# Weight splits moved off GpSimd, index steps charged less, the last selection's ends on GpSimd, masks one block ahead, chained minima

## The chip, the cores and the metric

The kernel runs as one program on one core of a Trainium2 chip. The metric is the device time of one execution in microseconds (us). TensorE does the matmuls, VectorE (DVE), ScalarE (ACT) and GpSimd (POOL) the element-wise work, and SyncE (SP) issues most of the transfers.

## The reference

One residual block on x (1 x 2048 x 1024, float32). A joint projection gives queries, a shared latent key and value, the indexer's queries, weights and keys, the pooling branch's input and two gates. For each block of 128 queries the indexer scores all admissible keys, and attention sees the 256 best alone:

```python
rel = jax.nn.relu(jnp.einsum('bqhd,bsd->bqhs', qib, k_idx).astype(jnp.float32) * idx_scale)
idx_score = jnp.einsum('bqh,bqhs->bqs', wib.astype(jnp.float32) * head_w_scale, rel)
idx_score = jnp.where(admissible[None], idx_score, -jnp.inf)
_, sel = lax.top_k(idx_score, topk)
...
s = jnp.einsum('bqhd,bqkd->bqhk', qb, k_sel).astype(jnp.float32) * attn_scale
p = jax.nn.softmax(s, axis=-1).astype(v_sel.dtype)
...
branch_a = attn @ w_attn_branch[l]
branch_b = multiscale_pool(pool_in, w_pool[l], pool_scale[l]) @ w_pool_branch[l]
gate_a, gate_b = jnp.split(jax.nn.sigmoid(gate_logits), 2, axis=-1)
mixed = (gate_a * branch_a + gate_b * branch_b) @ w_out[l]
x = layer_norm(ALPHA * x + mixed, ln1_g[l], ln1_b[l])
ffn = conv_ffn(x, conv_w[l], conv_b[l], w_ffn_up[l], w_ffn_down[l])
x = layer_norm(ALPHA * x + ffn, ln2_g[l], ln2_b[l])
```

There are 8 heads of 128 latent dimensions, 16 query blocks, and chunks of 64 frames; a query sees the keys of its own and of earlier chunks.

## The kernel before

**Matmuls.** Each float32 product is three matmuls: an operand is split into a rounded part `hi` and a rest `lo`, and `mm3` adds hi·hi, hi·lo and lo·hi. A split is two operations: a cast (`hi`) and a subtraction (`lo = src - hi`). `split` puts the cast on ACT and the subtraction on VectorE, or with `pool=True` both on GpSimd.

**Stages, in the order of the program.** The 2048 rows are four groups g of 512 (four blocks of 128 each). `proj_index` makes the indexer's and the latent projections of all groups (7.8 to 219.6 us). Then, for each group, `proj_pool`, `proj_q` and `proj_gates` (with `pool_map` inside): row group 0 from 219.6 to 438.9, group 1 to 664.2, group 2 to 902.5, group 3 to 1083.6. Attention runs over 32 units (g, h), a row group and a head each: those of group 0 until 1130.5, of group 1 until 1224.9, of group 2 until 1407, of group 3 until 1589.6. Then come `mix_out` (to 1870), `ffn_up` (to 2742) and `ffn_down`.

**Weights.** `self.ab` holds the projections' weights as tiles of 128x1024. The first row group loads each raw tile, splits it and stores both parts to DRAM; the later groups load the finished parts. In `get(i)`, tiles i+1 and i+2 are being loaded while tile i+1 is split. `self.ab` is made with the default `pool=True`, so its splits are on GpSimd: 32 tiles, of which 2 fall before 219.6 and 30 into the stage of row group 0.

**The background.** Index scores and selection are generators in `self.bg`, for the groups (0, 1), (2,) and (3,). After each step of the main program `turn` lets them go on as long as the modelled backlog of VectorE and ACT over TensorE (class `Clocks`) is under `SLACK`, and as long as there is credit, which grows by `RATE` = 0.75 of TensorE's modelled time and is charged by each step's modelled time on VectorE or ACT, whichever is longer. All of this is decided when the program is written out, so the order of instructions on each engine is fixed.

**Selection.** `index_scores` adds up the heads' scores of a block, one step for a head and a span. `select` then searches the 256th largest score of each row by bisecting over 32 bits, for two halves of the blocks in turn: a count on VectorE (`cd`, a compare that adds up), a sign sum on ACT (`ca`), and three small steps in `decide` (`g`, `h`, `F`) on 2 or 4 columns. The end of each block handles ties: ACT writes signs `sg` (f16), VectorE compares them with zero (`eq`), scans (`cu`), compares the scan with the number wanted, subtracts, and writes the mask (bf16, 0 or `MASKED`), which goes to DRAM through `self.stores`. The last selection is that of group 3, blocks 12 to 15 with 1664, 1792, 1920 and 2048 columns.

**Attention.** `load_unit(u + 1)` is called at the start of unit u's scores. For the first unit of a group it calls `load_masks(g)`: for each block of the group, `self.selected < b` steps the background by force until the mask is there, `settle` issues the waiting stores, and the mask is loaded; masks 0 and 1 are memsets on GpSimd. In `scores`, for each block rb and each chunk of up to 1024 keys, VectorE adds the mask to the scores in PSUM and takes the row maximum into `mx`; for a block of two chunks the maxima are joined and scaled by one operation on a column, for a block of one chunk they are scaled, and a memset clears the second sum. ACT then takes the exponential. `split_q(u + 1)` (on GpSimd) comes at the third block of a unit.

## Time and profile before

| | before |
|---|---|
| median of 3 runs | 3179.35 us (3173.73 to 3184.88) |
| profiled execution | 3178.85 us, span 3177.1 us |
| mean granted TensorE clock | 0.986 of full speed |
| TensorE busy | 3042.5 us (96%) |
| VectorE busy | 2486.0 us (78%) |
| ACT busy | 1587.3 us (50%) |
| GpSimd busy | 644.4 us (20%) |

Busy times are those of the one profiled execution; they overlap, and are means over stages that differ. The span is the time between the first and the last instruction on the core.

### The profile page before, as it was taken

How to read it: one execution, taken by the hardware profiler on the slowest of the kernel's cores; microseconds unless marked ns; L12 is line 12 of the kernel's file. 1: busy time of each engine (PE TensorE's matmuls, PEld its weight loads, DVE VectorE, ACT ScalarE, POOL GpSimd, SP SyncE). 2: the span in 40 equal slices, each digit the busy share in tenths (PEclk: the TensorE clock that was granted, in tenths of full speed). 3: DMA queues.
4: the chain of work that ended last, by engine and by line, in shares of the span. 5: the costliest groups of instructions: out<-in, count | busy, mean ns of one | idle time of the engine just before them, and what ended most of it. 6: DMA issues, size and time to landing. Idle time of an engine off the chain costs nothing. (4 is left out here: it accounts for less than half of the span.)

```text
span 3177.1 us, 44106 instructions
## 1 busy us (share of the span) xinstructions
PE 3042.5 (96%) x14750; PEld 2534.0 (80%) x14750; DVE 2486.0 (78%) x4737; ACT 1587.3 (50%) x3051; POOL 644.4 (20%) x592
## 2 busy tenths in 40 slices
PE   8988899999999999779999999999999999999998
PEld 8886688888888888668877777888778888888886
DVE  4589987987699989988876578999986655657776
ACT  3465656874578877657711134444443222433253
POOL 2027520010010221101231234545411111100011
PEclk9999899999999999989999999999999999999999
DMA  6658784756367332131254778888888866998753
GB/s 248 238 190 277 252 322 147 271 209 222 119 246 274 112 107 82 59 107 54 80 207 171 256 271 284 295 295 286 303 298 321 318 216 220 363 399 327 266 192 110
DMA packets 325841, 715.89 MB, mean 225 GB/s; under 512 B 27434, under 2 KB 132334, under 8 KB 325614
## 3 DMA queue, kind: packets, MB, share of 16 engines
q1 hardware_dynamic: 316974, 697.34, 61.9%
q10 hardware_dynamic: 8640, 15.73, 1.3%
q8 instruction: 117, 1.92, 0.2%
q14 instruction: 110, 0.90, 0.1%
HBM read 454.85 MB, written 258.11 MB: 224 GB/s over the span
## 5 line engine op out<-in xcount | busy, mean ns | idle before, releaser
L133 PE MATMUL p<-b,b 128*128 128x512 f32 (+3 forms) x12568 | 2825.4, 381 | 92.0 <-ACT b L133 32.0
L133 PEld LDWEIGHTS p<-b,b 128*128 128x128 f32 x12568 | 2254.6, 190 | 534.5 <-ACT b L133 35.6
L133 DVE TENSOR_TENSOR b<-p,b 128x512 f32<-128x512 f32 (+3 forms) x622 | 393.4, 655 | 154.6 <-PE p L133 98.1
L133 ACT ACTIVATE b<-p 128x512 fp32r<-128x512 f32 (+11 forms) x634 | 360.7, 603 | 280.6 <-PE p L133 268.9
L133 ACT ACTIVATE m<-b,F 128x448 bf16<-128x448 f32 (+3 forms) x448 | 366.2, 820 | 89.6 <-DVE F L133 70.9
L133 ACT ACTIVATE b<-b 128x512 fp32r<-128x512 f32 (+3 forms) x310 | 237.7, 784 | 325.6 <-DVE b L133 140.9
L133 DVE TENSOR_SCALAR_CACHE_REDUCE m<-b,F 128x512 bf16<-128x512 f32 (+6 forms) x476 | 370.1, 808 | 1.0
L133 DVE TENSOR_TENSOR b<-b,b 128x1024 fp32r<-128x1024 f32 (+6 forms) x268 | 302.9, 1141 | 76.0 <-DMA b<-h 29.9
L133 POOL TENSOR_TENSOR b<-b,b 128x1024 f32<-128x1024 f32 (+3 forms) x94 | 226.8, 2415 | 493.1 <-DVE b L133 339.8
L133 DVE SCALAR_TENSOR_TENSOR b<-b,cw,b 128x1023 f32<-128x1023 f32 (+1 forms) x176 | 246.3, 1412 | 69.7 <-ACT b L133 68.7
L133 ACT ACTIVATE b<-m 128x512 fp32r<-128x512 f32 x215 | 133.2, 628 | 334.7 <-DVE m L133 123.1
L133 ACT ACTIVATE b<-b,cw 128x1024 f32<-128x1024 f32 x88 | 106.9, 1236 | 269.9 <-DVE b L133 269.9
L133 ACT ACTIVATE b<-b,mx 128x1024 f32<-128x1024 f32 (+2 forms) x192 | 171.6, 896 | 73.0 <-DVE mx L133 71.2
L133 PE MATMUL p<-ident,b 128*128 128x128 f32 x1248 | 194.5, 274 | 9.6 <-DVE b L133 7.2
L133 DVE SCALAR_TENSOR_TENSOR b<-b,ws,b 128x768 f32<-128x768 f32 (+5 forms) x154 | 155.6, 1039 | 49.1 <-ACT b L133 46.8
L133 DVE CUSTOM_DVE_ANT_0 b<-p,b 128x1024 f32<-128x1024 f32 (+2 forms) x192 | 173.7, 907 | 20.9 <-PE p L133 19.9
L133 DVE TENSOR_TENSOR b<-m,b 128x512 fp32r<-128x512 f32 x215 | 151.2, 711 | 49.0 <-ACT b L133 48.8
L133 PEld LDWEIGHTS p<-ident,b 128*128 128x128 f32 x1248 | 152.4, 141 | 43.4 <-DVE b L133 5.1
L133 PE MATMUL p<-kst,b 128*128 128x384 f32 (+3 forms) x656 | 149.7, 359 | 6.8 <-DVE b L133 4.6
L133 ACT ACTIVATE m<-p 128x512 f32<-128x512 f32 (+2 forms) x172 | 100.8, 586 | 74.4 <-PE p L133 69.6
L133 PEld LDWEIGHTS p<-kst,b 128*128 128x128 f32 x656 | 111.9, 189 | 28.5 <-ACT b L133 13.7
L133 POOL TENSOR_SCALAR b<-b 128x1024 fp32r<-128x1024 f32 (+2 forms) x50 | 53.1, 1065 | 352.1 <-DMA b<-in_w_in_dram 184.9
(126 smaller groups left out, 1628.2 us busy)
## 6 DMA issues: line engine op xcount, KB each, us to landing
b<-wk SPq DMA_DIRECT2D x339, 512.0 KB
wk<-b SPq DMA_DIRECT2D x211, 512.0 KB
b<-h SPq DMA_DIRECT2D x88, 512.0 KB
b<-in_w_ffn_up_dram SPq DMA_DIRECT2D x44, 512.0 KB
h<-b SPq DMA_DIRECT2D x44, 512.0 KB
b<-vv SPq DMA_DIRECT2D x80, 256.0 KB
hs<-b SPq DMA_DIRECT2D x33, 512.0 KB
b<-hs SPq DMA_DIRECT2D x33, 512.0 KB
```

The source lines that it names most:

```text
L133: return f(*args, **kw)
```

## The change

- `self.ab` is made with `pool=False`: the first row group's weights are split by ACT (cast) and VectorE (subtraction).
- The steps of `index_scores` yield `LIGHT`, and `turn` charges such a step `RATE / INDEX_RATE`, 0.79 of its modelled time. This moves the background's later steps too.
- `select` gets the engine of the ends' element-wise operations: GpSimd for the selection of group 3, VectorE for the others. The scan, and the two operations on one column behind it, stay on VectorE.
- `load_masks(g)` becomes `load_mask(b)`: a block's mask is asked for while the block ahead of it is scored, in the first unit of a group, or for a group's first block in the last unit of the group before.
- The row maxima become minima of negated scores: the reduction scales by -`SCALE` and starts from the value of the chunk before, so that its last value is the bias of the exponential. The operation that joined and scaled them, the memset of the second sum, and for blocks of one chunk the addition of the two sums are gone.

```diff
--- before.py
+++ after.py
@@ -68,8 +68,10 @@
 NFIRST = 1
 FINE = "fine"
 PAUSE = "pause"
+LIGHT = "light"
 GRAIN = 1
 RATE = 0.75
+INDEX_RATE = 0.95
 CAP = 1.5
 EARLY = 2
 SWITCH = "A--"
@@ -449,7 +451,8 @@
                 self.bg.pop(0)
             if step == PAUSE:
                 break
-            self.credit -= max(work["dve"] - before["dve"], work["act"] - before["act"])
+            spent = max(work["dve"] - before["dve"], work["act"] - before["act"])
+            self.credit -= spent * (RATE / INDEX_RATE if step == LIGHT else 1.0)
 
     def run_to_end(self, gen):
         for step in gen:
@@ -548,7 +551,7 @@
         self.nab = len(specs) // NG
-        self.ab = Weights(self, specs, period=self.nab)
+        self.ab = Weights(self, specs, pool=False, period=self.nab)
 
 
     def load_x(self, g, n=DC // 2):
@@ -1042,11 +1045,11 @@
                         nc.vector.tensor_scalar(tiles[t], rl, wsc, None, op0=OP.mult)
                     else:
                         nc.vector.scalar_tensor_tensor(tiles[t], rl, wsc, tiles[t], op0=OP.mult, op1=OP.add)
-                    yield
+                    yield LIGHT
...
-    def select(self, halves):
+    def select(self, halves, ties):
@@ -1138,17 +1141,17 @@
                 nc.scalar.activation(sg[:, :N - w], front[b], AF.Sign, bias=tn[:, i:i + 1])
                 nc.scalar.activation(sg[:, N - w:], back[b], AF.Sign, bias=tn[:, i:i + 1])
                 yield
-                nc.vector.tensor_scalar(eq, sg, 0.0, None, op0=OP.is_equal)
+                ties.tensor_scalar(eq, sg, 0.0, None, op0=OP.is_equal)
                 nc.vector.tensor_tensor_scan(cu, eq, eq, 0.0, op0=OP.add, op1=OP.max)
                 nd = self.sml([P, 1], tag="nd")
                 nc.vector.scalar_tensor_tensor(nd, cu[:, N - 1:N], fx[:, i:i + 1], cg[:, i:i + 1],
                                                op0=OP.mult, op1=OP.subtract)
                 nc.vector.tensor_scalar(nd, nd, float(TOPK), None, op0=OP.add)
                 yield
-                nc.vector.tensor_scalar(eq, cu, nd, None, op0=OP.is_gt)
-                nc.vector.tensor_tensor(sg, sg, eq, op=OP.subtract)
+                ties.tensor_scalar(eq, cu, nd, None, op0=OP.is_gt)
+                ties.tensor_tensor(sg, sg, eq, op=OP.subtract)
                 m = self.T([P, N], BF16)
-                nc.vector.tensor_scalar(m, sg, -0.25, MASKED, op0=OP.is_lt, op1=OP.mult)
+                ties.tensor_scalar(m, sg, -0.25, MASKED, op0=OP.is_lt, op1=OP.mult)
                 self.store(self.d_msk[b], m)
                 del self.I[b]
                 self.selected = max(self.selected, b)
@@ -1169,28 +1172,26 @@
         self.kh, self.kl = [a, e], [b, f]
         self.masks, self.vv = {}, {}
 
-    def load_masks(self, g):
-        nc = self.nc
-        t = []
-        for b in range(g * RB, (g + 1) * RB):
-            m = self.T([P, P * (b + 1)], BF16)
-            if b < 2:
-                nc.gpsimd.memset(m, 0.0)
-                nc.gpsimd.memset(m[0:64, P * (b + 1) - 64:], MASKED)
-            else:
-                while self.selected < b:
-                    if next(self.bg[0][1], "end") == "end":
-                        self.bg.pop(0)
-                self.settle()
-                nc.sync.dma_start(m, self.d_msk[b])
-            t.append(m)
-        self.masks[g] = t
+    def load_mask(self, b):
+
+        nc = self.nc
+        if b >= NB or b in self.masks:
+            return
+        m = self.T([P, P * (b + 1)], BF16)
+        if b < 2:
+            nc.gpsimd.memset(m, 0.0)
+            nc.gpsimd.memset(m[0:64, P * (b + 1) - 64:], MASKED)
+        else:
+            while self.selected < b:
+                if next(self.bg[0][1], "end") == "end":
+                    self.bg.pop(0)
+            self.settle()
+            nc.sync.dma_start(m, self.d_msk[b])
+        self.masks[b] = m
 
     def load_unit(self, u):
 
         g, h = self.units[u]
-        if g not in self.masks:
-            self.load_masks(g)
         q = self.M([P, G])
         self.nc.sync.dma_start(q, self.d_q[g][:, h * ROT:(h + 1) * ROT])
         self.qraw[u] = q
@@ -1213,6 +1214,7 @@
         nc = self.nc
         g, h = self.units[u]
         if u == 0:
+            self.load_mask(0)
             self.load_unit(0)
             self.split_q(0)
         if u + 1 < len(self.units):
@@ -1224,7 +1226,9 @@
             b = g * RB + rb
             N = P * (b + 1)
             npc = (N + 1023) // 1024
-            m = self.masks[g][rb]
+            m = self.masks[b]
+            if h == 0 and rb < RB - 1 or h == H - 1 and rb == RB - 1:
+                self.load_mask(b + 1)
             if rb == 2 and u + 1 < len(self.units):
                 self.split_q(u + 1)
             qh, ql = (qs[:, i, rb * P:(rb + 1) * P] for i in range(2))
@@ -1236,25 +1240,25 @@
                     cw = min(512, n - c)
                     self.mm3(ps[:, c:c + cw], qh, ql, self.kh[pc][:, c:c + cw], self.kl[pc][:, c:c + cw], True, True)
                 s = self.T([P, n])
-                nc.vector.tensor_tensor_reduce(s, ps[:, :n], m[:, pc * 1024:pc * 1024 + n], scale=1.0, scalar=-3e38,
-                                               op0=OP.add, op1=OP.max, accum_out=mx[:, pc:pc + 1])
+                nc.vector.tensor_tensor_reduce(s, ps[:, :n], m[:, pc * 1024:pc * 1024 + n], scale=-SCALE,
+                                               scalar=mx[:, pc - 1:pc] if pc else 3e38,
+                                               op0=OP.add, op1=OP.min, accum_out=mx[:, pc:pc + 1])
                 ps_.append((s, n))
                 if pc < npc - 1:
                     yield n / (4.0 * P)
-            if npc == 2:
-                nc.vector.tensor_scalar(mx[:, 0:1], mx[:, 0:1], mx[:, 1:2], -SCALE, op0=OP.max, op1=OP.mult)
-            else:
-                nc.vector.tensor_scalar(mx[:, 0:1], mx[:, 0:1], -SCALE, None, op0=OP.mult)
-                nc.vector.memset(st["sum"][:, rb, 1:2], 0.0)
             for pc, (s, n) in enumerate(ps_):
-                nc.scalar.activation(s, s, AF.Exp, bias=mx[:, 0:1], scale=SCALE, accum_out=st["sum"][:, rb, pc:pc + 1])
+                nc.scalar.activation(s, s, AF.Exp, bias=mx[:, npc - 1:npc], scale=-1.0, accum_out=st["sum"][:, rb, pc:pc + 1])
             st["p"].append([s for s, _ in ps_])
             yield n / (4.0 * P)
         r = st["r"] = self.sml([P, RB], tag="rinv", bufs=10)
-        nc.vector.tensor_tensor(r, st["sum"][:, :, 0], st["sum"][:, :, 1], op=OP.add)
-        nc.vector.reciprocal(r, r)
+        if npc == 2:
+            nc.vector.tensor_tensor(r, st["sum"][:, :, 0], st["sum"][:, :, 1], op=OP.add)
+            nc.vector.reciprocal(r, r)
+        else:
+            nc.vector.reciprocal(r, st["sum"][:, :, 0])
         if h == H - 1:
-            del self.masks[g]
+            for b in range(g * RB, (g + 1) * RB):
+                del self.masks[b]
 
     def values(self, u):
 
@@ -2014,7 +2018,7 @@
             yield from self.index_scores(g)
         blocks = [b for g in groups for b in range(g * RB, (g + 1) * RB) if b >= 2]
         h = len(blocks) // 2 if len(blocks) < 4 else 2
-        yield from self.select([blocks[:h], blocks[h:]])
+        yield from self.select([blocks[:h], blocks[h:]], self.nc.gpsimd if groups[-1] == NG - 1 else self.nc.vector)
 
     def run(self):
         self.rows, self.wi_parts, self.keyed, self.selected = {}, [], -1, 1
```

What moves is shown at three places. In the rows, `b` are large tiles, `m` middle ones, `msk71` to `msk74` the masks of blocks 12 to 15 in DRAM, `q`, `vv`, `at` and `gm` queries, values, attention's output and gates in DRAM.

On SP in attention, before, around the start of group 3 (the value loads of unit 22, then the masks):

```order
L1204 DMA b4762_15750<-vv12_113 128x512
L1204 DMA b4763_15753<-vv13_114 128x512
L461 DMA msk71_172<-b4816_15962 128x1664
L1195 DMA m4846_16041<-q54_155 128x1x512
L1185 DMA b4815_15959<-msk71_172 128x1664
L461 DMA msk72_173<-b4822_15979 128x1792
L1185 DMA b4817_15966<-msk72_173 128x1792
L461 DMA msk73_174<-b4839_16020 128x1920
L1185 DMA b4823_15983<-msk73_174 128x1920
L461 DMA msk74_175<-b4845_16037 128x2048
```

and in the changed program at the start of attention, then, as the second piece, at the start of group 3:

```order
L1196 DMA m3944_12642<-q51_152 128x1x512
L1196 DMA m3946_12647<-q51_152 128x1x512
L464 DMA msk71_172<-b3939_12632 128x1664
L1205 DMA b3947_12649<-vv11_112 128x512
L1196 DMA m3970_12732<-q51_152 128x1x512
L1189 DMA b3953_12663<-msk61_162 128x384
L1189 DMA b3957_12674<-msk62_163 128x512
L1196 DMA m3993_12792<-q51_152 128x1x512
```

```order
L1205 DMA b4844_15866<-vv13_114 128x512
L1189 DMA b4883_16021<-msk71_172 128x1664
L1196 DMA m4896_16075<-q54_155 128x1x512
L464 DMA at77_178<-m4882_16017 128x512
L1205 DMA b4897_16077<-vv11_112 128x512
L1205 DMA b4897_16077<-vv12_113 128x512
L1205 DMA b4898_16080<-vv13_114 128x512
L1205 DMA b4898_16080<-vv14_115 128x512
L1189 DMA b4900_16084<-msk72_173 128x1792
L1189 DMA b4912_16131<-msk73_174 128x1920
```

The stores of the four last masks no longer stand between their own loads: that of block 12 stands ahead of the loads of masks 2 and 3, and the loads of masks 12 to 15 are apart, with other transfers between them.

On GpSimd at the start of attention, before (`b3851` and `b3852` split the latent keys, the memsets write masks 0 and 1, the rows on `m` split queries):

```order
L133 TENSOR_SCALAR b3851_12415<-b3795_12240 128x1024
L133 TENSOR_TENSOR b3852_12416<-b3795_12240,b3851_12415 128x1024
L133 MEMSET b3885_12525 128x128
L133 MEMSET b3886_12528 128x256
L133 MEMSET b3885_12525 64x64
L133 MEMSET b3886_12528 64x64
L133 TENSOR_SCALAR b3900_12565<-m3891_12540 128x512
L133 TENSOR_TENSOR b3900_12565<-m3891_12540,b3900_12565 128x512
```

and in the changed program:

```order
L135 TENSOR_SCALAR b3922_12544<-b3867_12368 128x1024
L135 TENSOR_TENSOR b3923_12545<-b3867_12368,b3922_12544 128x1024
L135 TENSOR_SCALAR b3934_12594<-b3933_12593 128x1664
L135 TENSOR_SCALAR b3934_12594<-b3935_12595,nd3938_12615 128x1664
L135 TENSOR_TENSOR b3933_12593<-b3933_12593,b3934_12594 128x1664
L135 TENSOR_SCALAR b3939_12632<-b3933_12593 128x1664
L135 MEMSET b3943_12639 128x128
L135 MEMSET b3943_12639 64x64
L135 MEMSET b3949_12652 128x256
L135 MEMSET b3949_12652 64x64
L135 TENSOR_SCALAR b3958_12676<-m3946_12647 128x512
L135 TENSOR_TENSOR b3958_12676<-m3946_12647,b3958_12676 128x512
L135 TENSOR_SCALAR b3941_12635<-b3940_12634 128x1792
```

The four element-wise operations of block 12's end stand ahead of the memsets of masks 0 and 1 and of the first query split; the first comparison of block 13 is behind that split.

On GpSimd in the stage of row group 0, before (rows of 128x1024 are splits of weights, the others belong to the pooling windows):

```order
L133 TENSOR_TENSOR b1090_3666<-b1028_3496,b1089_3665 128x1024
L133 TENSOR_SCALAR b1091_3669<-b1029_3498 128x1024
L133 TENSOR_TENSOR b1092_3670<-b1029_3498,b1091_3669 128x1024
L133 TENSOR_SCALAR b1157_3849<-b1087_3661 128x1024
L133 TENSOR_TENSOR b1158_3850<-b1087_3661,b1157_3849 128x1024
L133 TENSOR_SCALAR b1159_3853<-b1088_3663 128x1024
```

and on VectorE in the same stage, in the changed program (rows with `cd` are the search's counts; `g`, `h` and `F` its small steps):

```order
L135 TENSOR_SCALAR m1059_3553,cd1056_3550<-b628_1927,F1048_3515 128x128
L135 SCALAR_TENSOR_TENSOR g1060_3556<-cd1042_3507,ca1043_3508 128x4
L135 TENSOR_SCALAR h1061_3557<-g1060_3556 128x4
L135 SCALAR_TENSOR_TENSOR F1062_3558<-h1061_3557,F1039_3493 128x4
L135 TENSOR_SCALAR m1075_3590,cd1056_3550<-b650_2005,F1048_3515 128x256
L135 TENSOR_TENSOR b1066_3565<-b995_3381,b1065_3564 128x1024
L135 SCALAR_TENSOR_TENSOR g1080_3601<-cd1056_3550,ca1057_3551 128x2
L135 TENSOR_SCALAR m1079_3598,cd1076_3595<-b677_2132,F1062_3558 128x192
L135 TENSOR_TENSOR b1068_3569<-b996_3383,b1067_3568 128x1024
L135 TENSOR_SCALAR m1084_3612,cd1076_3595<-b747_2446,F1062_3558 128x320
L135 TENSOR_SCALAR h1081_3602<-g1080_3601 128x2
L135 TENSOR_SCALAR m1086_3617,cd1076_3595<-b779_2586,F1062_3558 128x448
L135 SCALAR_TENSOR_TENSOR F1082_3603<-h1081_3602,F1048_3515 128x2
```

The subtractions of the weights' splits now stand between the counts of the search on VectorE; their casts stand on ACT between the search's sign steps.

## Rows read from the trace of the kernel before

**Rows 1.** Windows by stage: window, length; busy us (count) by engine; PE clock, DMA share, GB/s.

```profile
90.90:219.60 128.70, 117.81 (x835) 110.49 (x834) 84.73 (x190) 66.02 (x130) 9.09 (x6) 0.97 0.54 182
219.60:438.90 219.30, 192.64 (x814) 152.74 (x813) 202.46 (x637) 142.57 (x428) 120.42 (x92) 0.95 0.82 287
461.60:532.10 70.50, 70.50 (x353) 59.02 (x352) 49.65 (x68) 32.28 (x49) 14.17 (x11) 1.00 0.48 171
902.50:1083.60 181.10, 180.66 (x807) 149.47 (x806) 169.90 (x433) 146.59 (x270) 20.09 (x26) 1.00 0.60 213
1083.60:1224.90 141.30, 136.88 (x826) 115.32 (x824) 121.96 (x382) 107.46 (x249) 36.43 (x48) 1.00 0.37 112
1224.90:1370.40 145.50, 109.59 (x624) 90.37 (x625) 137.30 (x293) 92.35 (x194) 14.77 (x18) 0.88 0.22 67
1370.40:1571.90 201.50, 200.40 (x1188) 170.99 (x1186) 171.86 (x342) 148.76 (x287) 20.73 (x27) 1.00 0.24 75
```

**Rows 2.** A window inside the stretch 1224.90 to 1370.40, same columns.

```profile
1340.00:1370.00 30.00, 2.96 (x7) 2.11 (x7) 27.73 (x38) 6.26 (x8) 2.80 (x2) 0.50 0.28 97
```

**Rows 3.** TensorE's timeline there: start, us, operation, count, [idle before, what ended it].

```profile
1367.73 2.90 PE L133 MATMUL p<-b,b 128*128 128x512 f32 x6 [17.16 <-DVE mx L133]
```

**Rows 4.** SP's timeline there: transfers issued.

```profile
1336.33 0.32 SPq L461 DMA_DIRECT2D msk<-b  x1
1338.91 0.31 SPq L1185 DMA_DIRECT2D b<-msk  x1
```

**Rows 5.** TensorE's waits in row group 0's stage: us, times, longest.

```profile
PE p L133 <- ACT m L133: 13.0, 6, 3.7
PE p L133 <- POOL b L133: 9.6, 9, 2.1
```

**Rows 6.** VectorE's forms in row group 0's stage: busy us, mean ns, idle before.

```profile
L133 DVE SCALAR_TENSOR_TENSOR F<-h,F 128x4 int32<-128x4 int32 x31 | 23.3, 752 | 0.5
L133 DVE SCALAR_TENSOR_TENSOR F<-h,F 128x2 int32<-128x2 int32 x31 | 18.5, 597 | 1.0
L133 DVE SCALAR_TENSOR_TENSOR g<-cd,ca 128x4 f32<-128x4 f32 x32 | 17.6, 551 | 4.2 <-ACT m L133 3.6
L133 DVE SCALAR_TENSOR_TENSOR g<-cd,ca 128x2 f32<-128x2 f32 x31 | 11.0, 356 | 1.3 <-ACT m L133 1.1
L133 DVE TENSOR_SCALAR h<-g 128x4 int32<-128x4 f32 x32 | 12.0, 375 | 1.0
L133 DVE TENSOR_SCALAR_CACHE_REDUCE m<-b,F 128x320 bf16<-128x320 f32 x31 | 16.7, 538 | 0.0
```

**Rows 7.** VectorE's forms from 532 to 1075 us.

```profile
L133 DVE SCALAR_TENSOR_TENSOR F<-h,F 128x2 int32<-128x2 int32 x119 | 24.2, 203 | 3.8
L133 DVE SCALAR_TENSOR_TENSOR g<-cd,ca 128x2 f32<-128x2 f32 x124 | 21.8, 175 | 7.7 <-ACT m L133 4.0
L133 DVE TENSOR_SCALAR h<-g 128x2 int32<-128x2 f32 x123 | 21.5, 175 | 3.6
L133 DVE TENSOR_TENSOR b<-b,b 128x1024 fp32r<-128x1024 f32 x1 | 1.2, 1225 | 0.0
```

**Rows 8.** Timeline around 309 us, all engines.

```profile
308.93 2.40 POOL L133 TENSOR_TENSOR b<-b,b 128x1024 fp32r<-128x1024 f32 x1
309.17 2.18 DVE L133 SCALAR_TENSOR_TENSOR F<-h,F 128x4 int32<-128x4 int32 x1
```

**Rows 9.** GpSimd's forms in row group 0's stage.

```profile
L133 POOL TENSOR_TENSOR b<-b,b 128x1024 fp32r<-128x1024 f32 x30 | 72.4, 2415 | 2.3
L133 POOL TENSOR_SCALAR b<-b 128x1024 fp32r<-128x1024 f32 x30 | 31.6, 1053 | 64.5 <-DMA b<-in_w_in_dram 46.3 <-DMA gm<-m 12.2 <-DMA b<-in_w_pool_branch_dram 6.0
```

**Rows 10.** ACT's casts of 128x1024 before 220 us.

```profile
L133 ACT ACTIVATE b<-b 128x1024 fp32r<-128x1024 f32 x17 | 17.4, 1053 | 6.2 <-DMA b<-in_xT_dram 5.7 <-DMA b<-in_w_in_dram 0.5
```

**Rows 11.** VectorE's timeline in block 12's end: the scan and the subtraction.

```profile
1313.48 3.62 DVE L133 TENSOR_TENSOR_SCAN b<-b 128x1664 f16<-128x1664 f16 x1
1322.85 1.02 DVE L133 TENSOR_TENSOR b<-b,b 128x1664 f16<-128x1664 f16 x1
```

## The prediction

> **What bounds the kernel now.** I read first the windows by stage, which say where TensorE stands still, then the waits, the forms and the timelines inside the two stages that came out. Where nothing special happens TensorE is the bound: the projections of group 3 take 181.10 us with 180.66 of TensorE busy, and group 3's attention 201.50 with 200.40 [rows 1]. Two stages stand out. The projections of row group 0 do the same work as those of group 3, but take 219.30 us: 192.64 busy at a clock of 0.95, 26.7 idle [rows 1]. And the stretch 1224.90 to 1370.40 takes 145.50 with 109.59 busy, 35.9 idle, at a clock of 0.88 [rows 1]. Together that is 62.6 us of idle time; the rest of this text is about which part comes back, and what the change puts in its place.
>
> **The second stretch: the forced ends of the last selection.** The hole is 1340 to 1370: TensorE 2.96 of 30 us, VectorE 27.73, granted clock 0.50, the lower level (1.2 GHz), while TensorE hardly works [rows 2]. TensorE's last wait there is 17.16 us for a maximum `mx`, that is for VectorE [rows 3]. SP shows why: a mask is stored at 1336.33 and loaded again at 1338.91, 2.6 us later, and so on for the next three [rows 4], because `load_masks(3)` runs the four ends of the last selection one behind the other and puts them ahead of the scores on VectorE. In the changed order the ends of blocks 12 and 13 stand at the start of attention and those of 14 and 15 in group 1, and none is forced. With them go the 35.9 idle and some microseconds at the low clock; a little stays, since masks still come through DRAM. Term: **-37**, bounds -30 and -40.
>
> **The first stretch: 30 weight splits leave GpSimd.** TensorE waits there 13.0 us for ACT `m` (the evictions, queued behind the search's sign steps) and 9.6 us for POOL `b` (split weights) [rows 5]. On VectorE the small steps of the search are what to look at: the 128x4 form of `F` takes 752 ns, that of `g` 551, that of `h` 375 [rows 6]; after this stage the same operations take 203, 175 and 175 [rows 7]. On so few columns I price the 4-column and the 2-column forms alike: F 62 x 0.203, g 63 x 0.175 and the 128x4 h 32 x 0.175 make 29 us, against the 82.4 us that these five rows add up to [rows 6, 7]. 53 us of VectorE's 202.46 are thus waiting inside instructions. One instance shows for what: an `F` begins at 309.17 and lasts 2.18 us, while GpSimd's subtraction of 2.40 us runs from 308.93; both end at 311.3 [rows 8].
>
> The Trainium skill (SBUF — State Buffer, "Who interferes with whom") states that a VectorE instruction with two inputs in SBUF and a GpSimd instruction that reads SBUF exclude each other for a whole instruction. The trace agrees: 2.18 us in place of 0.203 [rows 7, 8].
>
> The change takes the 30 subtractions (2.415 us) and 30 casts (1.053) from GpSimd [rows 9], puts the casts on ACT at 1.053 each [rows 10] and the subtractions on VectorE at 1.225 each, from the one that the trace has there [rows 7]. By the order, 14 counts (some 0.54 us each, [rows 6]) and 12 small steps also leave this stage for an earlier one, about 10 us. VectorE: 202.5 - 53 + 36.8 - 10 = 176 us; ACT: 142.6 + 31.6 = 174 at most [rows 1]. Both lie below the 181 to 187 us that TensorE needs, but close. The DMA share of 0.82 is 180 us of 219.3 [rows 1], and GpSimd's casts waited 46.3 us for `in_w_in` [rows 9]; on ACT such a wait now holds evictions. The gap to group 3's stage is 38.2 us. I take two thirds of it, since three engines at 93% of the new stage cannot be in step: **-25**. Bounds: -36 (all but the start) and -10 (ACT's waits for weights in place of GpSimd's).
>
> **The ends of blocks 12 and 13, now at the start of attention, on GpSimd.** No row has a comparison of GpSimd on f16. By its float32 rows of 128x1024, one block of 1664 columns costs (3 x 1.053 + 2.415) x 1.625 = 9.05 us [rows 9], with VectorE's scan of 3.62 us in its middle [rows 11]; VectorE alone took 1.02 us for the subtraction [rows 11] that these rows put at 3.9. Behind this chain of 13 us stand, on GpSimd, the memset of mask 0 and the q splits; on SP, behind the store of mask 12, the values and masks 2 and 3 of unit 0. Below, what TensorE has in hand covers most of it: +2. Above, the chain and a store and load of 2.6 us [rows 4] show nearly whole: +15. I take the middle, **+8**.
>
> **The ends of blocks 14 and 15, in group 1's units.** Chains of (3 x 1.053 + 2.415) x 1.875 and x 2 are 10.5 and 11.1 us [rows 9] in a stretch in which VectorE is busy 121.96 of 141.30 us [rows 1]. Each stands in front of a unit's `split_q` on GpSimd, and its two scans of about 4 us (3.62 by the columns, [rows 11]) in front of score reductions. GpSimd is idle for 105 of these 141 us [rows 1], which covers all but the place in the queue: **+5**, bounds 0 and +10.
>
> **Masks one block ahead.** A load now stands on SP in the middle of a unit, behind a settle that sends waiting stores first; what is queued behind are q and value loads. The masks were stored long before, so one such wait is no store's landing. **+3**, bounds 0 and +6.
>
> **Index scores charged at 0.79.** They begin sooner: in the last two index stages, where VectorE is busy 84.73 of 128.70, about 14 counts and 12 small steps come in, some 10 us; in the q projection of group 1, 14 more accumulations of about 0.9 us beside 49.65 of 70.50 [rows 1]. Both have cover (44 and 21 us). **0**; without that cover +8, and -4 if idle TensorE time before 219.6 takes index matmuls (10.9 us are there [rows 1]).
>
> **Chained minima.** 128 operations on one column and 64 memsets less on VectorE. In group 3 TensorE is busy 200.40 of 201.50 with VectorE at 171.86 [rows 1], so nothing shows: **0**, bounds -3 and +2, the latter as each second chunk now waits for the first one's minimum.
>
> **Sum.** The profiled execution took 3178.85 us (span 3177.1), half a microsecond under the median. 3178.85 - 37 - 25 + 8 + 5 + 3 = 3132.9; I say **3132**. The measurement tells 0.3%, 9.5 us, from no change.
>
> **Rivals.** (a) The first stage gives little. ACT in order waits for weights and then runs casts and sign steps while evictions stand; VectorE is loaded as before. For it: DMA share 0.82, the 46.3 us; against it: 53 us of VectorE set free. First term -5 in place of -25: **3152**. Chance 0.18.
> (b) All comes back. Both holes close and the ends cost nothing, as each has half a unit of lead: -40 - 36 + 5 for the masks and ends, **3108**. Against it: a forced store and load before unit 0. Chance 0.12.
> (c) The exclusion seen in [rows 8] moves with the work. Each GpSimd chain reads SBUF, and VectorE's scan and its two-input steps wait for it, or it for them. Four chains by the rows are 5.57 x (1.625 + 1.75 + 1.875 + 2) = 40 us; if a third more of them reaches TensorE, +14: **3146**. Against it: the score reductions of attention read one input from PSUM, and nothing shows that these wait. Chance 0.08. The page named above speaks for this rival, as the scan has its two inputs in SBUF; no run here shows a scan beside GpSimd.
> (d) The other side: the comparisons on f16 run far off the float32 rows. If every added microsecond of these 40 holds TensorE through GpSimd's queue, the 56 us between 3132 and 3188 are used up where an operation takes 2.4 times its row; at three times it is 3132 + 80 = **3212**. Against it: the float32 rows of this engine go by columns. Chance 0.04.
> (e) The change does not act: an end is still forced at group 3, and the first stage stays as long. The order excludes the first, not the sum of small losses: **3178**. Chance 0.03.
>
> The forecast has the remaining 0.55, with 3118 to 3146 as its own range. The range for 8 in 10 is 3109 to 3162: below it lies half of (b) (0.06), above it (d), (e) and a quarter of (a), where the bounds of the ends and masks at their worse values (+18) come on top (0.12 together). Faster: 0.55 + 0.18 + 0.12 + 0.08 = 0.93; same 0.04, (e) and the slight end of (d); slower 0.03.
>
> **What would show it.** Right: no TensorE idle of over 5 us between 1200 and 1400; the stage of row group 0 at 190 to 200 us, with `F` at about 0.2 us; GpSimd's comparisons at 1.6 to 2.2 us; idle TensorE time of some 5 to 10 us around the start of attention. Wrong: waits for ACT `b` (weights) of over 15 us in the first stage (a), `F` or scans that end together with GpSimd's comparisons (c), or a hole at the first units while GpSimd runs one comparison (d).

## The result, and the profile after

The change makes the kernel slower: 3211.76 us median (3208.75 to 3216.11) against 3177.6 of the kernel before (four runs; three of them gave the 3179.35 above), a ratio of 1.0103 (95% interval 1.0091 to 1.0116). The forecast was 3132, with a range of 3109 to 3162. Here and below a ratio and its interval are estimated from all runs, so they differ by up to 0.001 from the quotient of two medians.

Windows by stage of the changed kernel, columns and order as in [rows 1]: the last index stages, row groups 0 and 1, group 3's projections with the start of attention, the units of group 0, of group 1 and of group 2.

```profile
89.80:224.70 134.90, 121.07 (x835) 110.80 (x833) 89.39 (x226) 75.17 (x157) 1.61 (x4) 0.97 0.49 167
224.70:440.70 216.00, 191.43 (x814) 153.58 (x813) 177.59 (x650) 162.78 (x433) 20.04 (x30) 0.94 0.84 295
440.70:675.70 235.00, 228.33 (x1061) 189.13 (x1061) 196.20 (x479) 155.49 (x301) 15.64 (x21) 0.98 0.62 225
915.70:1116.90 201.20, 183.66 (x808) 151.14 (x807) 165.66 (x412) 136.01 (x248) 41.91 (x30) 0.96 0.54 195
1116.90:1185.30 68.40, 46.76 (x263) 40.24 (x262) 57.14 (x130) 37.34 (x104) 33.83 (x28) 0.80 0.33 99
1185.30:1301.70 116.40, 98.39 (x564) 83.18 (x564) 88.35 (x169) 76.02 (x150) 64.65 (x32) 0.93 0.32 94
1301.70:1442.70 141.00, 140.85 (x843) 120.46 (x842) 118.91 (x248) 110.47 (x232) 18.31 (x24) 1.00 0.27 85
```

The forced hole is gone: in the last window TensorE is busy 140.85 of 141.00. The stage of row group 0 hardly shrank (219.30 before), and the start of attention and group 1's units grew by some 60 us, with GpSimd busy 33.83 and 64.65. TensorE's timeline there, the rows with the long waits:

```profile
238.37 1.83 PE L135 MATMUL p<-ident,m 128*128 128x128 f32 x6 [8.01 <-ACT ws L135]
...
356.51 1.65 PE L135 MATMUL p<-b,wpool 128*128 128x512 f32 x3 [6.52 <-ACT m L135]
361.68 1.65 PE L135 MATMUL p<-b,wpool 128*128 128x512 f32 x3 [3.52 <-ACT m L135]
596.16 1.65 PE L135 MATMUL p<-b,wpool 128*128 128x512 f32 x3 [5.79 <-ACT m L135]
...
1109.52 5.21 PE L135 MATMUL p<-b,b 128*128 128x384 f32 x14 [12.80 <-DVE mx L135]
...
1138.98 4.96 PE L135 MATMUL p<-b,b 128*128 128x256 f32 x15 [13.56 <-DVE mx L135]
...
1256.78 1.12 PE L135 MATMUL p<-ident,b 128*128 128x128 f32 x4 [8.30 <-DVE b L135]
...
1287.78 2.93 PE L135 MATMUL p<-b,b 128*128 128x512 f32 x6 [6.94 <-DVE mx L135]
```

The waits from 1109 on have their source on GpSimd. Its timeline: the end of block 12.

```profile
1085.80 4.45 POOL L135 TENSOR_SCALAR b<-b 128x1664 f16<-128x1664 f16 x1 [28.80 <-ACT b L135]
1094.52 4.83 POOL L135 TENSOR_SCALAR b<-b,nd 128x1664 f16<-128x1664 f16 x1 [4.27 <-DVE nd L135]
1099.43 3.32 POOL L135 TENSOR_TENSOR b<-b,b 128x1664 f16<-128x1664 f16 x1
1102.84 5.83 POOL L135 TENSOR_SCALAR b<-b 128x1664 bf16<-128x1664 f16 x1
1108.72 0.85 POOL L135 MEMSET b<- 128x128 bf16 x4
```

A comparison takes 4.45 us and the mask 5.83, where the forecast had 1.71 for each from [rows 9]; the subtraction takes 3.32, less than the 3.92 forecast. The four operations are 18.4 us against 9.05; with the scan the memset of mask 0 begins 22.9 us after the first comparison. VectorE's timeline of the same stretch, with two rows of GpSimd between:

```profile
1090.28 3.62 DVE L135 TENSOR_TENSOR_SCAN b<-b 128x1664 f16<-128x1664 f16 x1 [6.52 <-POOL b L135]
...
1109.16 0.29 DVE L135 CUSTOM_DVE_ANT_0 b<-p,b 128x128 f32<-128x128 f32 x1 [13.10 <-POOL b L135]
...
1127.71 3.56 POOL L135 TENSOR_TENSOR b<-b,b 128x1792 f16<-128x1792 f16 x1
1127.88 3.41 DVE L135 TENSOR_TENSOR t<-F,st 128x2 f32<-128x2 f32 x1
...
1131.37 6.24 POOL L135 TENSOR_SCALAR b<-b 128x1792 bf16<-128x1792 f16 x1
1131.53 6.10 DVE L135 TENSOR_SCALAR ab<-ab 128x2 f32<-128x2 f32 x1
```

Three things hold VectorE: its scan waits in order for the comparison (6.52), a score reduction waits for mask 0 (13.10), and operations on two columns last 3.41 and 6.10 us, beginning just behind an operation of GpSimd and ending with it.

### The profile page after: what moved, and what is told of

It reads as the page before. It is cut to its first block, busy times and chain, and to the rows that moved or that the text cites. A ratio compares the mean times of both kernels' runs of the same rounds, so it can differ in the third digit from the quotient of the medians.

```text
span 3207.0 us, 43930 instructions
## 1 busy us (share of the span) xinstructions
PE 3049.6 (95%) x14750; PEld 2540.8 (79%) x14750; DVE 2448.3 (76%) x4545; ACT 1620.9 (51%) x3083; POOL 620.1 (19%) x544
## 5 line engine op out<-in xcount | busy, mean ns | idle before, releaser
L135 ACT ACTIVATE b<-b 128x512 fp32r<-128x512 f32 (+3 forms) x342 | 271.0, 809 | 333.4 <-DVE b L135 162.6
L135 DVE TENSOR_TENSOR b<-b,b 128x1024 fp32r<-128x1024 f32 (+5 forms) x296 | 337.0, 1149 | 88.8 <-ACT b L135 39.1
L135 POOL TENSOR_TENSOR b<-b,b 128x1024 f32<-128x1024 f32 (+5 forms) x66 | 164.9, 2500 | 489.1 <-DVE b L135 318.9
L135 PE MATMUL p<-ident,b 128*128 128x128 f32 x1248 | 196.3, 276 | 13.6 <-DVE b L135 11.5
L135 DVE CUSTOM_DVE_ANT_0 b<-p,b 128x1024 f32<-128x1024 f32 (+7 forms) x128 | 125.9, 986 | 73.1 <-PE p L135 43.6
L135 POOL TENSOR_SCALAR b<-b 128x1024 fp32r<-128x1024 f32 (+10 forms) x26 | 65.3, 2518 | 193.8 <-PE p L135 129.5
```

Source lines behind the costliest of these rows:

```text
L135: return f(*args, **kw)
```

## The experiments

To say where a kernel loses or wins, the table gives how much later (us) TensorE's first matmul of a stage comes than in the kernel before, in the profiled executions. The columns: the projections of groups 0, 1 and 2 (219.6, 438.9 and 664.2 before), attention's units 1, 8, 16 and 24 (1087.3, 1130.5, 1224.9 and 1407.1), and last the difference of the medians, each against the runs of the kernel before that belong to it. A profiled execution need not be the median one: that of kernel 14 is its fastest, 8 us under its median, that of 5 lies 4.7 above, the others within 3.5.

| kernel | g0 | g1 | g2 | u1 | u8 | u16 | u24 | time |
|---|---|---|---|---|---|---|---|---|
| changed | 5.1 | 1.8 | 11.5 | 52.5 | 54.8 | 76.8 | 35.6 | +34.2 |
| 1 ends on VectorE | 7.8 | 4.5 | 14.2 | 26.5 | 34.7 | 35.9 | 7.5 | +4.0 |
| 2 splits only | -5.4 | -16.8 | -16.6 | -13.2 | -13.4 | -13.5 | -3.2 | -9.0 |
| 3 as 1, splits back | 10.9 | 16.4 | 31.9 | 43.1 | 47.5 | 57.9 | 18.8 | +16.3 |
| 4 pacing only | 11.2 | 16.1 | 29.5 | 40.4 | 38.0 | 37.6 | 13.1 | +13.5 |
| 5 as 1, no pacing | -5.0 | -16.7 | -16.4 | -8.0 | -7.3 | -6.6 | -6.5 | -14.1 |
| 6 as 1, pacing from group 2 | -5.9 | -17.5 | -10.8 | -6.5 | -2.3 | -0.6 | -17.1 | -17.3 |
| 7 as 6, at 1.2 | -3.6 | -12.8 | -4.1 | 11.4 | 16.8 | 17.6 | -9.9 | -10.6 |
| 9 queue cleared | 6.0 | 2.5 | 12.1 | 42.0 | 53.1 | 73.7 | 33.0 | +29.9 |
| 10 minima only | -0.7 | -2.1 | -1.7 | -0.9 | -3.5 | -1.9 | -5.3 | -6.5 |
| 11 masks only | -0.2 | -0.6 | -0.3 | 0.5 | 5.0 | 4.2 | 2.1 | +4.2 |
| 12 rate 0.85 from group 2 | -7.5 | -18.7 | -18.4 | 20.4 | 22.7 | 28.4 | -7.3 | -5.0 |
| 13 both queues cleared | 7.8 | 4.3 | 14.0 | 39.8 | 47.5 | 68.5 | 27.3 | +25.1 |
| 14 as 6, splits back | -2.3 | -3.8 | 3.6 | 8.2 | 12.1 | 16.8 | -11.7 | -5.9 |
| 15 rate 0.80 from group 2 | -5.8 | -17.4 | -17.1 | -8.5 | -5.7 | -3.5 | -17.8 | -18.4 |

**1, the ends on VectorE.** In the changed kernel:

```diff
-        yield from self.select([blocks[:h], blocks[h:]], self.nc.gpsimd if groups[-1] == NG - 1 else self.nc.vector)
+        yield from self.select([blocks[:h], blocks[h:]], self.nc.vector)
```

> The changed kernel, with all four operations of the last selection's ends on VectorE again; everything else as changed. Theory (the engine: GpSimd's comparisons take 2.7 to 3.5 ns a column, and hold the memset of mask 0, the query splits and VectorE's small steps): the 39 us lost at the start of attention and the 20 us lost in group 1's units go, but for some 5 to 8 us, 3152 to 3165 us. Rival (the place: scan, store and load ahead of unit 0 cost as much on any engine): 3185 to 3205 us.

3183.19 us, ratio 1.0016 (1.0007 to 1.0026): the engine is worth 28.6 us of the change. That is less than the theory's 47 to 60, and just below the rival's 3185 to 3205: from the start of group 3's projections (15.9 late) to unit 1 (26.5) and unit 8 (34.7) some 19 us are still lost with the ends on VectorE. Not all of that is the place of the ends. Kernels 5, 6, 11 and 15 have no end there and lose 4 to 11 us over the same stretch (5 with the masks alone, in 11), so that the place itself is left with 8 to 15.

**2, the splits only**, in the kernel before, and **3**, the splits taken back in the kernel of the first experiment:

```diff
-        self.ab = Weights(self, specs, period=self.nab)
+        self.ab = Weights(self, specs, pool=False, period=self.nab)
```

> The kernel before, with the first row group's weight splits on ACT and VectorE; nothing else changed. As forecast (VectorE freed of some 50 us of waiting inside instructions, two thirds of the idle time back): 3150 to 3158 us. Theory now (ACT's casts wait in order for weight transfers and the evictions at the pooling map still stand behind sign steps, so the holes move but stay): 3170 to 3182 us.

> The first experiment's kernel (ends on VectorE), with the first row group's weight splits on GpSimd again. If the split's move gives what was forecast: 20 to 25 us above the first experiment's time. If it gives nothing: within 6 us of it.

2: 3170.19, ratio 0.9973 (0.9963 to 0.9983), at the edge of the second theory. 3: 3195.43, 12.2 above the first, between its two expectations. So the splits give 9 to 12 us. The table shows more, 17 us by group 1, but in the second experiment they melt to 3 at unit 24. Its window at the forced hole shows why:

```profile
1307.30:1366.00 58.70, 17.74 (x89) 13.52 (x88) 54.19 (x93) 20.88 (x37) 2.84 (x2) 0.65 0.18 62
```

VectorE is busy 54.19 of 58.70 us: by this it sets when the hole ends, and TensorE's earlier arrival only makes the wait longer. Units 16 to 24 take 10 us more than in the kernel before.

**4, the pacing only**, in the kernel before (`yield LIGHT` and the charge of 0.79), and **5**, all but the pacing, in the kernel of the first experiment:

```diff
-INDEX_RATE = 0.95
+INDEX_RATE = 0.75
```

> The kernel before, with only the index steps charged at 0.79. The ends of blocks 12 to 14 then come unforced, that of block 15 alone is forced. Theory (the 36 us hole of the forced ends is what pacing is worth, less some microseconds for ends at the start of attention and for fuller index stages): 3145 to 3160 us. Rival (what the earlier background adds in the index stages, in group 1's projections and at the start of attention eats it): 3170 to 3180 us.

> The changed kernel with index steps charged in full again (0.75) and the ends on VectorE: left of the change are the splits, the masks one block ahead and the chained minima, beside the second experiment's splits alone (3170 us). The ends of blocks 13 to 15 are forced again, but one block at a time. If masks and minima give nothing: 3166 to 3174 us. If asking for one mask at a time spreads the forced ends over four score steps and so shortens their hole: 3140 to 3160 us.

4: 3192.64, ratio 1.0047 (1.0030 to 1.0063), slower, and beyond even the rival's 3170 to 3180. 5: 3165.24, ratio 0.9965 (0.9952 to 0.9978), against 3183.19 with the pacing; it is just below the range for masks and minima that give nothing, and far from that of a shorter hole. Both say that the pacing costs 13 to 18 us. Kernels 1 and 5 differ in it alone: 31 us of loss by group 2's projections (14.2 against -16.4), 43 by unit 16, and 29 given back at the hole that is no longer there.

**6, 7: pacing from group 2 on**, in the kernel of the first experiment; 7 has `INDEX_RATE = 1.2` too:

```diff
-                    yield LIGHT
+                    yield LIGHT if g >= 2 else None
```

> The first experiment's kernel (ends on VectorE), with index steps charged less for groups 2 and 3 alone, so that the index stages and the projections of groups 0 and 1 go as before. Theory (the pacing's loss of some 30 us comes from the first background, in which the index stages, the attention's row group 1 and the pooling maps had no room; group 2's and 3's projections have room): the 11 to 15 us at the index stages and the 10 us at group 1's pooling map go, 3150 to 3165 us, with some of the forced hole back. Rival (the background's work only moves its price to where it runs): within 8 us of the first experiment's 3183.

> As the run before it, with the charge of groups 2 and 3 lowered to 0.75/1.2, which puts the four ends where the changed kernel has them, none forced. Theory: no hole at the ends, and the early stages as before, 3145 to 3160 us; the rival: 3175 or more, as group 2's projections or the start of attention take over what the hole gave.

6: 3162.0, ratio 0.9948 (0.9930 to 0.9966), as the theory had it. 7: 3168.69, ratio 0.9962 (0.9948 to 0.9975), between the two: the hole is gone, but the ends of blocks 12 and 13 are back at the start of attention, and units 1 to 16 are 18 us later than in 6.

**8, the prices of GpSimd.** Behind the last store of the kernel before, three times over (`h` f16, `f` float32, `bm` bf16, all 128x1024; lines 2069 to 2079):

```diff
+            gp.tensor_scalar(h2, h1, 0.0, None, op0=OP.is_equal)
+            gp.tensor_scalar(h2, h1, col, None, op0=OP.is_gt)
+            gp.tensor_scalar(bm, h1, -0.25, MASKED, op0=OP.is_lt, op1=OP.mult)
+            gp.tensor_scalar(h2, h1, 2.0, None, op0=OP.mult)
+            gp.tensor_scalar(h2, h1, 2.0, 1.0, op0=OP.mult, op1=OP.mult)
+            gp.tensor_scalar(f2, f1, 0.0, None, op0=OP.is_equal)
+            gp.tensor_scalar(f2, f1, -0.25, MASKED, op0=OP.is_lt, op1=OP.mult)
+            gp.tensor_scalar(f2, f1, 2.0, None, op0=OP.mult)
+            gp.tensor_scalar(f2, f1, 2.0, 1.0, op0=OP.mult, op1=OP.mult)
+            gp.tensor_tensor(h2, h1, h1, op=OP.subtract)
+            gp.tensor_tensor(f2, f1, f1, op=OP.subtract)
```

> The kernel before, with a list of GpSimd operations of 128x1024 added behind its last store, three times over: comparisons and multiplications, on f16 and on float32, and the subtraction on both. If the comparison makes the price (2.7 to 3.5 ns a column in the changed kernel): float32 comparisons take 2.7 us or more too, f16 multiplications about 1.05. If the f16 operands make it: float32 comparisons take about 1.05 us and f16 multiplications 2.7. The time grows by the list, some 50 to 70 us.

GpSimd's forms of that kernel:

```profile
L2071 POOL TENSOR_SCALAR b<-b 128x1024 bf16<-128x1024 f16 x3 | 11.7, 3892 | 0.2
L2075 POOL TENSOR_SCALAR b<-b 128x1024 f32<-128x1024 f32 x3 | 11.1, 3683 | 0.2
L2070 POOL TENSOR_SCALAR b<-b,nd 128x1024 f16<-128x1024 f16 x3 | 8.6, 2854 | 0.1
L2074 POOL TENSOR_SCALAR b<-b 128x1024 f32<-128x1024 f32 x3 | 8.4, 2790 | 0.0
L2072 POOL TENSOR_SCALAR b<-b 128x1024 f16<-128x1024 f16 x3 | 8.3, 2779 | 0.2
L2076 POOL TENSOR_SCALAR b<-b 128x1024 f32<-128x1024 f32 x3 | 8.3, 2779 | 0.0
...
L2073 POOL TENSOR_SCALAR b<-b 128x1024 f16<-128x1024 f16 x3 | 3.2, 1050 | 0.1
L2077 POOL TENSOR_SCALAR b<-b 128x1024 f32<-128x1024 f32 x3 | 3.1, 1049 | 0.1
```

The time is 3249.59 us, not to be compared. Both expectations were wrong. The type matters little and the comparison does not: a single multiplication takes 2779 ns like a single comparison, and a comparison with a multiplication behind it 3.7 to 3.9 us. What is cheap, at 1050 ns in both types, is the pair of two multiplications, and that is the form in which the kernel before writes its casts (`1.0, 1.0, mult, mult`).

**9, 13: the queues at the start of attention.** 9 is the changed kernel with the memsets of masks 0 and 1 on VectorE and the first query splits on ACT and VectorE. 13 also lets GpSimd issue the stores of the last masks:

```diff
-            nc.gpsimd.memset(m, 0.0)
-            nc.gpsimd.memset(m[0:64, P * (b + 1) - 64:], MASKED)
+            nc.vector.memset(m, 0.0)
+            nc.vector.memset(m[0:64, P * (b + 1) - 64:], MASKED)
...
-        self.split(qs[:, 0], qs[:, 1], self.qraw.pop(u), pool=u > 0)
+        self.split(qs[:, 0], qs[:, 1], self.qraw.pop(u), pool=u > 4)
```

```diff
-                self.store(self.d_msk[b], m)
+                if ties is nc.vector:
+                    self.store(self.d_msk[b], m)
+                else:
+                    nc.gpsimd.dma_start(self.d_msk[b], m)
```

> The changed kernel, with what stood behind block 12's and 13's ends on GpSimd at the start of attention taken off it: the memsets of masks 0 and 1 on VectorE, the first four query splits after unit 0 on ACT and VectorE. The ends stay on GpSimd. Theory (two causes: GpSimd's queue holds TensorE once for some 13 us, and the comparisons hold VectorE's small steps, which costs a second hole of some 13 us): the first hole goes, the second stays, 3195 to 3203 us. Rival (the queue is all): both go, 3180 to 3190 us. Rival (the queue is nothing): 3207 or more.

> The ninth experiment's kernel, with the stores of the last selection's masks issued by GpSimd itself, so that SP's loads no longer stand behind them. Theory (SP's queue holds the loads of masks 2 and 3 until the chain of block 12 has ended): the first hole of some 14 us goes, the time is 3188 to 3197 us. Rival (VectorE is held by GpSimd's comparisons whatever the queues do): 3200 or more.

9: 3206.14, near the rival that the queue is nothing; its ratio 1.0099 (1.0084 to 1.0114) is not told apart from the change's. VectorE's timeline and then SP's say what took over:

```profile
1116.29 0.56 DVE L135 CUSTOM_DVE_ANT_0 b<-p,b 128x384 f32<-128x384 f32 x1 [16.47 <-DMA b<-msk]
...
1109.54 0.32 SPq L464 DMA_DIRECT2D msk<-b  x1
...
1111.07 0.93 SPq L1189 DMA_DIRECT2D b<-msk  x2
```

VectorE now waits 16.47 us for mask 2, whose load stands on SP behind the store of mask 12. With that store gone too, 13 comes to 3202.22, ratio 1.0077 (1.0062 to 1.0092): the two edits together are worth 9 us, and the rival (3200 or more) held. VectorE's timeline of 13 shows the rest:

```profile
1105.50 4.21 DVE L135 TENSOR_TENSOR b<-m,b 128x512 fp32r<-128x512 f32 x1
...
1116.77 3.89 DVE L135 TENSOR_TENSOR_SCAN b<-b 128x1792 f16<-128x1792 f16 x1 [6.45 <-POOL b L135]
```

A query split of 0.69 us elsewhere lasts 4.21 beside GpSimd's mask operation, and the next scan waits 6.45 us for its comparison, with score reductions behind it. How the remaining 20 us divide between these two was not tried. Nor do the 9 us price the queues by themselves: the edits put four query splits on VectorE beside GpSimd's chains, where they last 2.86 to 4.21 us each, some 11 us more than four of 0.69.

**10, 11: minima and masks alone**, in the kernel before: the edits of `scores` and of `load_mask` as in the change.

> The kernel before, with the chained minima alone. As forecast: nothing, 3175 to 3182 us. Rival (VectorE is the bound from 1225 to 1370 us, so 128 small operations and 64 memsets less come back there): 3166 to 3173 us.

> The kernel before, with the masks asked for one block ahead and nothing else; blocks 13 to 15 are still forced, but one at a time, between score steps. As forecast, a small loss: 3178 to 3186 us. Rival (forced ends spread over four score steps overlap with TensorE): 3155 to 3172 us.

10: 3169.7, ratio 0.9982 (0.9972 to 0.9991), within the rival's range. 11: 3180.46, ratio 1.0012 (1.0003 to 1.0022), as forecast.

**12, 15: another way to pace**, the index steps charged in full, the ends on VectorE, the rate raised from group 2's projections on (0.85 in 12, 0.80 in 15):

```diff
-        self.credit = min(self.credit + RATE * (pe - self.seen), CAP)
+        self.credit = min(self.credit + (RATE if self.stage < 2 else 0.80) * (pe - self.seen), CAP)
```

> The changed kernel with the ends on VectorE, index steps charged in full, and the rate at 0.85 in place of 0.75 from group 2's projections on, for all steps of the background. The index stages and groups 0 and 1 go as in the kernel before, and no end is forced; those of blocks 12 and 13 are at the start of attention. Theory (the early stages have no room, group 2's projections have): no hole at the ends, some 10 us lost at the start of attention, 3145 to 3160 us. Rival (work moved out of the hole costs as much where it goes): 3168 or more.

> The twelfth experiment's kernel with the rate at 0.80 in place of 0.85 from group 2's projections on. The ends of blocks 12 and 13 then lie in group 1's and early group 2's units, not at the start of attention, and block 15's is forced. Theory (the ends cost little inside the units and much at the start of attention): 3155 to 3163 us. Rival (the forced end of block 15 costs as much): 3168 or more.

12: 3171.2, ratio 0.9984 (0.9974 to 0.9993), as the rival had it: no hole, but 39 us lost from group 2's projections to unit 1, where the ends of blocks 12 and 13 stand. 15: 3158.68, ratio 0.9936 (0.9920 to 0.9953), as the theory had it and the best kernel here, with one end forced and none at the start of attention. Against kernel 5, from which only the rate tells it apart, it wins 4 to 7 us.

**14, the splits back** in the kernel of experiment 6:

> The sixth experiment's kernel (3162 us) with the first row group's weight splits on GpSimd again. If the forced hole took what the splits had won: 15 to 19 us more, 3177 to 3181. If VectorE's load in attention takes it even without forced ends: 7 to 12 us more, 3169 to 3174.

3171.18, 9.2 above the sixth (11.4 with each against its own runs of the kernel before): the splits' gain shrinks also where hardly an end is forced. By the table 17 us of it are there up to unit 16 and 5 at unit 24. It supports VectorE's load in attention as the taker, but it is no sharp test: the runs of this kernel lie far apart (3162.84 to 3176.99), and with the splits back the background moves too, so that the scan of block 12 comes at 1087.7, at the start of attention, in place of 1175.5.

## Why the prediction was wrong, point by point

Three terms failed: the price of the ends' operations on GpSimd, the pacing at nothing, and the splits at two thirds of the gap. That the forced hole goes was right.

- **The forced ends: -37.** Right for the hole: from unit 16 to unit 24 the changed kernel wins 41 us (76.8 to 35.6 late). But this holds no longer where the ends of blocks 14 and 15 come later. In kernel 1 their scans are at 1263.4 and 1323.0, behind the start of unit 16 (1260.8), and the same units win 28, though no end is forced. In the changed kernel (1221.2 and 1251.7) they were paid for ahead of it.
- **The splits: -25.** Less than half of it, 9 to 12. VectorE came out as worked out, 177.59 us against 176, and `F`, `g` and `h` at 0.16 to 0.20 us, so the steps no longer wait inside GpSimd's subtractions. But VectorE's 53 us were not what TensorE waited for. In kernel 2, the splits alone, the waits for POOL `b` of [rows 5] are gone, and those for ACT stay, 14.6 us against 13.0:

```profile
PE p L135 <- ACT m L135: 14.6, 3, 7.4
```

  The pooling map's hole is most of it: evictions still stand behind sign steps on ACT, which the casts filled further (162.78 us in the changed kernel). So the stage gives 11 us where the term had 25. With the pacing beside it rival (a)'s wait came as well, in one place:

```profile
234.56 1.06 ACT L135 ACTIVATE b<-b 128x1024 fp32r<-128x1024 f32 x1 [11.69 <-DMA b<-in_w_in_dram]
```

  A cast waits 11.69 us for its weights, and TensorE 8.01 behind it. Alone, the splits win 17 us by group 1 (5 of them ahead of the stage), and half of that is gone by the end, as it seems to VectorE's load in attention. Two steps failed: the two thirds of the gap, taken from the loads of the engines though TensorE waits for ACT's order, and the addition, since a gain ahead of a stretch in which another engine sets the pace is not kept.
- **Block 12's to 15's ends on GpSimd: +8 and +5.** The largest error. Price: the row taken for the comparisons was the pair of two multiplications, the only cheap form (experiment 8). By the trace the four chains take 80.5 us instead of 40. Effect: where +8 stood, from group 3's projections to unit 8, the changed kernel loses 42 us and kernel 1 loses 19; where +5 stood, in group 1's units, 22 and 1, with waits of 8.30 and 6.94 where the forecast had none over 5. By unit 24 some 13 of this difference have come back, and in the time the engine is worth 28.6 us; 8 to 15 more go with the place. The queues named in the forecast did hold (experiments 9 and 13), for 9 us as edited there; rival (c)'s waiting inside instructions is in the trace too, and so is a wait that the forecast did not list, VectorE's scan standing in order for GpSimd's comparison. Rival (d), with a chance of 0.04, had the price: 2.6 times the row for a comparison and 3.4 for the mask. That its 3212 is also the time measured is luck: it lays 80 us on the chains, of which engine and place took at most 44, and knows nothing of the pacing; and its reason, f16, is not the cause.
- **The pacing: 0.** Wrong by 31 us up to group 2's projections (1 against 5), in the index stages, at group 0's first projection and at group 1's pooling map (5.79 at 596.16), and by 13 to 18 in the time. I had taken VectorE's idle time as cover (44 and 21 us). But an engine idles in order, when its next operation waits for something. In the last index stages, the window and TensorE's waits (us, times, longest) of kernel 1, with the pacing, and then of kernel 5, without it:

```profile
89.40:227.40 138.00, 123.98 (x835) 113.77 (x834) 89.76 (x229) 75.24 (x157) 1.61 (x4) 0.95 0.48 163
PE p L135 <- ACT b L135: 8.3, 10, 1.9
PE p L135 <- DVE b L135: 5.5, 6, 1.7
...
89.60:214.50 124.90, 116.73 (x834) 109.19 (x833) 82.11 (x193) 67.68 (x132) 1.65 (x3) 0.99 0.55 188
PE p L135 <- ACT b L135: 5.3, 6, 1.8
PE p L135 <- DVE b L135: 2.5, 3, 1.4
```

  VectorE is busy 65% of the longer window, and yet TensorE waits 6 us more for it and ACT, in short pieces. Its busy time for the same matmuls grows by 7 us, at a mean granted clock of 0.95 in place of 0.99: the forecast had no term for that. Which of the added steps end these waits was not traced.

  That the steps are also cheaper in the planner's model than on the chip (0.07 + 640 x 0.00104 = 0.74 us for an accumulation of 640 columns, 884 ns as the mean of 22 in the trace of the kernel before) fits, but was not tried.
- **Masks +3**: measured +4.2. **Minima 0**: measured -6.5. Group 2's units were short of VectorE (137.30 busy of the 145.50 us from 1224.90 [rows 1]), so its work there was not hidden, which the choice of group 3 as the cover overlooked; by the table 3 us of it come there, the rest is not placed. The window taken for group 3's attention, 1370.40 to 1571.90, begins 37 us ahead of that group's units.
- **The sum.** Pacing +13.5, splits -9.0, masks +4.2, minima -6.5 and the engine of the ends +28.6 make +30.8; measured are +34.2. That is close, but the parts are not independent: the pacing is +13.5 alone and +18 beside the rest, the splits -9.0 and -12.2. What is shown is which terms failed and about what each is worth; that the sum comes so near is in part luck.

## What to carry to other kernels

A row prices an operation only if the operations inside it are the same: look at the arguments, not at the name in the row, and measure the form by itself before a chain is built on it. Idle time of an engine is no cover for in-order work unless one sees what ends that idle time. And where work is moved out of a hole, look first for the stretch that has room: the same lighter charge costs 13 to 18 us when it acts from the start, while from group 2 on it leaves the kernel 21 us faster than from the start (6 against 1).

## What the runs showed that I had not expected

GpSimd's operation with one tensor input and two multiplications takes 1.05 us for 1024 columns, and any other tried, a single multiplication too, 2.78 or more, on f16 as on float32. The Trainium skill (GPSIMD Engine Reference, "Engine selection") calls one-input operations there roughly line-rate; the trace agrees for the pair of multiplications alone (1.05 us, about 1 ns a column). And beside GpSimd an operation of VectorE on two columns with one input took 6.10 us, not only those with two inputs.
